# The last pair of chunks of a Strassen-type down projection joins the seven products, and the norms behind it are begun early

## The chip, the cores and the metric

One core of one Trainium2 chip. The metric is the device time of one execution in microseconds (us), the median of several; lower is better. Engines: PE (TensorE, matmuls), DVE (VectorE), ACT (ScalarE), POOL (GpSimd), SP (here only the queue that issues DMAs).

## The reference

One transformer block, S = 1024 tokens, D = 1024, DFF = 2816, in float32:

```python
f = _swiglu(_rmsnorm(x, ffn1_pre_g[l]), ffn1_w_gate[l], ffn1_w_up[l], ffn1_w_down[l])
x = x + 0.5 * _rmsnorm(f, ffn1_post_g[l])
h = _rmsnorm(x, mix_pre_g[l])
qkv = h @ w_qkv[l]
...
x = x + _rmsnorm(heads @ w_out[l], mix_post_g[l])
f = _swiglu(_rmsnorm(x, ffn2_pre_g[l]), ffn2_w_gate[l], ffn2_w_up[l], ffn2_w_down[l])
x = x + 0.5 * _rmsnorm(f, ffn2_post_g[l])
```

where `_swiglu(x, g, u, d) = (silu(x @ g) * (x @ u)) @ d`, and heads come from grouped-query attention and a dilated windowed attention, which the change does not touch.

## The kernel before

Every float32 factor is split into a high part in a short float type (ACT, L118) and a low rest (DVE or POOL, L119), and each product is three passes of matmuls (`PASSES`). The hidden width is cut into NF = 22 chunks of 128. The gate and up projections of a chunk go through seven products of a Strassen-Winograd scheme (P1 to P7, line 289). The down projection does the same over pairs of chunks: a pair j is a 2 x 2 block matrix (two chunks by two halves of the tokens) times a 2 x 2 block matrix of weights (b11, b12, b21, b22: two chunks by two column halves of the output). The seven products k = 0 to 6 of a pair are twelve matmuls 128x512 each, three for each of four rows i of 128 tokens (line 357). The ten pairs are done in two groups of five, all pairs of a group for k = 0, then all for k = 1, and so on, so that a product adds up in PSUM over the pairs of its group. One (k, j) is an *item*. At a group's end of product k its four rows are added into the token tiles y (T = i for the first half of the tokens, i + 4 for the second); `U`, the sum of products 0 and 2, is added into three blocks of y for each row, in the second group by twelve additions that are put off (`late`, L371) and let into DVE's queue one at a time as items are emitted.

For each item two 128x512 blocks are split (L118 and L119 on b, a weight block, and on h, a left block that comes back from DRAM), two items ahead (`WBUFS`). The weight combinations that the products need are made in place by POOL (L260 to L265), after the split that still reads the old block.

Chunks 20 and 21 stay out of the pairs. `tail` (L472) multiplies them plainly, token tile by token tile: twelve matmuls a tile, 96 in all, with T in the order 4, 5, 6, 7, 0, 1, 2, 3. In FFN1 the post norm (L542 to L544), the mixer's pre-norm (`mix_norm`, L480), the transposes into `actT` (L107 to L109) and the first two weights of the qkv projection (L568) run tile by tile behind it; in FFN2 the post norm and the store of the output (L1064) do.

A scheduler orders the instructions on each engine at build time; an engine runs its own in order.

Of the kernel before, what the change touches and what calls it, by code (L numbers as in the profile page):

```python
# [36 lines left out]
def tile_macaron_block(ctx, tc, x, f1_pre, f1_post, f1_g, f1_u, f1_d, mix_pre, mix_post, w_qkv,  # L37
# [83 lines left out]
    class Ffn:  # L121
# [17 lines left out]
        def __init__(self, wg, wu, wd, tag, far):  # L139
# [3 lines left out]
            self.A, self.Hs, self.S = {}, {}, {}  # L143
            self.items = [("G", i, p) for i in range(1, NF) for p in (self.ORDER if i < NF - 1 else self.LAST)]
            downs = [("D", k, j) for g in self.GROUPS for k in range(7) for j in g]
# [4 lines left out]
            self.tiles += [("N", c, d) for d in range(2) for c in range(2)]  # L150
            self.wanted = [d[1:] for d in downs] + [("h", i, h) for i in (NF - 2, NF - 1) for h in range(2)]
# [3 lines left out]
            self.made = self.used = self.done = 0  # L155
# [44 lines left out]
        def feed(self):  # L200

            while self.made < len(self.tiles) and self.made - self.used < self.WBUFS:
                it = self.tiles[self.made]
                self.made += 1
                {"G": self.prepare, "D": self.prepare_down, "N": self.prepare_last}[it[0]](*it[1:])
# [22 lines left out]
        def open_down(self):  # L228

            self.dw = open_pool("dw" + self.tag, bufs=len(self.GROUPS[0]), side=self.far)  # L230
            for j in self.GROUPS[0]:
                self.load_block(j, "b11")

        def load_block(self, j, name):
            c, b = divmod(self.BLOCKS.index(name), 2)
            r = self.B[j, name] = self.dw.tile([128, 512], F32, name=name)
            SP.dma_start(r, self.wd[128 * (2 * j + c):128 * (2 * j + c) + 128, 512 * b:512 * b + 512])
# [9 lines left out]
        def prepare_down(self, k, j, part):  # L247
# [6 lines left out]
            if k == 0 and j in self.GROUPS[0]:  # L254
                for b in ("b21", "b22", "b12"):
                    self.load_block(j, b)
            b11, b12, b21, b22 = [self.B[j, n] for n in self.BLOCKS]
# [8 lines left out]
            if k > 2:  # L266
                after = j + len(self.GROUPS[0])
                if after <= self.PAIRS:
                    self.load_block(after, {3: "b12", 4: "b21", 5: "b11", 6: "b22"}[k])
# [59 lines left out]
        def keep(self, j):  # L329

            a11, a21, a12, a22 = [self.H[2 * j + c][b] for c in range(2) for b in range(2)]
            s2, s3, s4 = [self.dn.tile([128, 512], F32, name="h") for _ in range(3)]
            for k, t in ((0, a11), (1, a12), (4, a22)):
                SP.dma_start(self.hd[k, j], t)
            for k, o, p, q, op in ((5, a21, a21, a22, OP.add), (2, s2, a21, a11, OP.subtract),
                                   (3, s3, a22, s2, OP.subtract), (6, s4, a12, s2, OP.subtract)):
                def made(k=k, o=o, p=p, q=q, op=op):
                    DVE.tensor_tensor(o, p, q, op=op)
                    SP.dma_start(self.hd[k, j], o)
                self.late.append(made)  # L340

        def down(self, k, j, y, ps, psd):
            A, B = [self.W[j, k, z].rearrange("p a k f -> p a (k f)") for z in range(2)]
            g = j in self.GROUPS[1]
            start, end = j == self.GROUPS[g][0], j == self.GROUPS[g][-1]
            first = k in (0, 2, 3, 5)
            U, add, tt = self.U, OP.add, DVE.tensor_tensor
            for i in range(4):
                if first and start:
                    if k in (0, 3):  # L350
                        self.Q[i] = psd.tile([128, 512], F32, name="pd")
                    else:
                        b = "abcd"[i]
                        self.Q[i] = ps[i // 2].tile([128, 4, 128], F32, name="p" + b).rearrange("p t f -> p (t f)")
                p = self.Q[i]
                for n, (a, b) in enumerate(PASSES):
                    PE.matmul(p, A[:, a, 128 * i:128 * i + 128], B[:, b, :],  # L357
                              start=(first and start and n == 0), stop=(end and n == 2), skip_group_check=True)
# [6 lines left out]
                if k == 0:  # L365
                    ACT.activation(U[:, i], p, AF.Copy)
                elif k == 2:
                    tt(U[:, i], U[:, i], p, op=add)
                    if g:
                        for v in (yv(i, 1), yv(i + 4, 0), yv(i + 4, 1)):  # L370
                            self.late.append(lambda v=v, i=i: tt(v, v, U[:, i], op=add))  # L371
                else:
# [5 lines left out]
                    else:  # L378
                        tt(v, U[:, i], p, op=add)

        def split_h(self):

            for i in (NF - 2, NF - 1):
                for half in range(2):
                    src = self.A.pop(("h", i, half))
                    hv, lv = [self.dn.tile([128, 512], FR, name="h") for _ in range(2)]
                    ACT.activation(hv, src, AF.Copy)
                    DVE.tensor_tensor(lv, src, f32(hv), op=OP.subtract)
# [749 lines left out]
```

## Time and profile before

| | |
|---|---|
| median of 3 runs | 2056.73 us (2054.08 to 2058.05) |
| the profiled execution | 2054.44 us, span 2052.7 us |
| mean granted TensorE clock | 0.992 |
| busy: PE, DVE, POOL, ACT | 1978.4, 1338.1, 1056.0, 1005.4 us |
| instructions on PE | 10728 |

The time is that of the whole execution, the span that from the first to the last instruction in the trace. An engine's busy time is the sum over its instructions; the granted clock is a share of full speed.

### The profile page before, as it was taken

Reading aid. Unit: us, or ns where it says so; the run is one execution under the profiler, and the core shown is the slowest. Engines: PE = TensorE matmul, PEld = TensorE weight load, DVE = VectorE, ACT = ScalarE, POOL = GpSimd, SP = SyncE. Lnnn points to the kernel's source line nnn. Section 1 sums busy time; section 2 is a strip of 40 time slices with the busy share of each in tenths; the row PEclk is TensorE's granted clock in tenths of the full one; section 3 lists DMA queues with packets and bytes.
Section 4 is the critical chain, followed back from the end, with each engine's and each line's share of the span. In section 5 each row is a group of like instructions: output and inputs, shape, how many; then the busy total and the mean of one; then the engine's idle time right before and its main releaser. Section 6 shows DMA issues by size and latency. Waiting matters only on the chain. (4 is left out here: it accounts for less than half of the span.)

```text
span 2052.7 us, 30441 instructions
## 1 busy us (share of the span) xinstructions
PE 1978.4 (96%) x10728; PEld 1675.0 (82%) x10728; DVE 1338.1 (65%) x2255; ACT 1005.4 (49%) x1892; POOL 1056.0 (51%) x894
## 2 busy tenths in 40 slices
PE   7999999999999699999999999999999999999995
PEld 6777777787888599998999998887777777778884
DVE  7655454557667846756999888356545445576688
ACT  5433333334444433436999999234333333344443
POOL 4566656666050604234777887315565665651504
PEclk9999999999999899999999999999999999999998
DMA  4233332326532542233040643322223233365434
GB/s 149 76 100 100 106 103 82 124 88 231 185 113 88 200 136 92 73 105 71 1 139 1 205 136 98 103 77 72 93 88 124 86 98 99 101 231 175 123 93 174
DMA packets 210681, 233.01 MB, mean 114 GB/s; under 512 B 21088, under 2 KB 147040, under 8 KB 210400
## 3 DMA queue, kind: packets, MB, share of 16 engines
q1 hardware_dynamic: 210528, 231.06, 35.8%
q8 instruction: 85, 1.39, 0.3%
q14 instruction: 68, 0.56, 0.1%
HBM read 164.95 MB, written 66.06 MB: 113 GB/s over the span
## 5 line engine op out<-in xcount | busy, mean ns | idle before, releaser
L119 POOL TENSOR_TENSOR wgu<-rawgu,wgu 128x512 fp32r<-128x512 f32 x216 | 315.5, 1469 | 354.2 <-ACT wgu L118 332.2
L118 ACT ACTIVATE wgu<-rawgu 128x512 fp32r<-128x512 f32 x302 | 181.7, 627 | 376.9 <-POOL rawgu L226 190.3
L289 PE MATMUL pa<-actT,wgu 128*128 128x512 f32 (+1 forms) x1080 | 268.7, 396 | 9.6 <-ACT U L410 8.7
L357 PE MATMUL pd<-wgu 128*128 128x512 f32 x1140 | 272.4, 391 | 2.5 <-DVE wgu L119 2.2
L357 PEld LDWEIGHTS pd<-wgu 128*128 128x128 f32 x1140 | 213.0, 188 | 51.5 <-DVE wgu L119 5.9
L289 PEld LDWEIGHTS pa<-actT,wgu 128*128 128x128 f32 x1080 | 197.7, 190 | 66.1 <-ACT U L410 21.9
L568 PE MATMUL pq<-wq,actT 128*128 128x256 f32 x1728 | 217.2, 284 | 0.7 <-ACT actT L108 0.7
L568 PEld LDWEIGHTS pq<-wq,actT 128*128 128x128 f32 x1728 | 208.5, 189 | 1.3 <-ACT actT L108 1.0
L118 ACT ACTIVATE wgu<-b 128x512 fp32r<-128x512 f32 x148 | 93.1, 631 | 203.3 <-PE pd L357 113.2
L119 DVE TENSOR_TENSOR wgu<-b,wgu 128x512 fp32r<-128x512 f32 x144 | 118.1, 821 | 98.9 <-ACT wgu L118 98.5
L768 POOL TENSOR_SCALAR P<-P,il 128x1024 f32<-128x1024 f32 (+1 forms) x128 | 130.4, 1018 | 64.9 <-DVE il L767 61.5
L447 DVE TENSOR_TENSOR h<-h,C 64x512 f32<-64x512 f32 x42 | 51.4, 1223 | 161.4 <-ACT h L446 161.3
L869 DVE TENSOR_TENSOR PT<-pt,PT 128x512 fp32r<-128x512 f32 (+1 forms) x256 | 146.3, 614 | 2.0 <-ACT PT L868 2.0
L289 PE MATMUL pd<-actT,wgu 128*128 128x512 f32 x552 | 136.3, 395 | 0.5 <-DVE U L418 0.5
L289 PE MATMUL pc<-actT,wgu 128*128 128x512 f32 x552 | 136.0, 395 | 0.0
L868 ACT ACTIVATE PT<-pt 128x512 fp32r<-128x512 f32 (+1 forms) x256 | 125.1, 543 | 10.7 <-PE pt L865 7.4
L865 PE MATMUL pt<-identr,P 128*128 128x128 f32 x896 | 125.1, 275 | 1.7 <-ACT vst L703 1.1
L289 PEld LDWEIGHTS pd<-actT,wgu 128*128 128x128 f32 x552 | 103.4, 188 | 26.2 <-DVE U L418 1.2
L289 PEld LDWEIGHTS pc<-actT,wgu 128*128 128x128 f32 x552 | 103.4, 188 | 24.9 <-DVE actT L109 0.3
L289 PE MATMUL pc<-tx,wgu 128*128 128x512 f32 x504 | 122.6, 392 | 0.0
L289 PE MATMUL pb<-tx,wgu 128*128 128x512 f32 x504 | 122.4, 391 | 0.0
L289 PE MATMUL pd<-tx,wgu 128*128 128x512 f32 x504 | 121.3, 390 | 0.0
(190 smaller groups left out, 3905.8 us busy)
## 6 DMA issues: line engine op xcount, KB each, us to landing
hd<-h SPq DMA_DIRECT2D x140, 256.0 KB, 2.9
h<-hd SPq DMA_DIRECT2D x140, 256.0 KB, 2.9
rawgu<-in_ffn_w_gate_dram SPq DMA_DIRECT2D x88, 256.0 KB, 3.0
rawgu<-in_ffn_w_up_dram SPq DMA_DIRECT2D x88, 256.0 KB, 3.5
b<-in_ffn_w_down_dram SPq DMA_DIRECT2D x88, 256.0 KB, 3.3
bkT<-kd SPq DMA_DIRECT2D x32, 320.0 KB, 7.5
rawq<-in_w_qkv_dram SPq DMA_DIRECT2D x16, 512.0 KB, 4.8
bV<-vd SPq DMA_DIRECT2D x8, 640.0 KB, 4.0
```

The lines of the kernel that those rows point to most:

```text
L118: ACT.activation(hi, raw, AF.Copy)
L119: return eng.tensor_tensor(lo, raw, f32(hi), op=OP.subtract).ins
L289: PE.matmul(p[:, c0:c1, :], w[:, a, k, :], self.rhs(name, b, k)[:, c0:c1, :], start=(first and n == 0), stop=(n == 11), skip_group_check=True)
L357: PE.matmul(p, A[:, a, 128 * i:128 * i + 128], B[:, b, :], start=(first and start and n == 0), stop=(end and n == 2), skip_group_check=True)
L447: DVE.tensor_tensor(dst, s[64:128], c[64:128], op=OP.mult)
L568: PE.matmul(p, actT[:, a, k, T, :], WQ[j][:, b, k, :], start=(n == 0), stop=(n == 23))
L768: POOL.tensor_scalar(P[:, 0:w], P[:, 0:w], il, 1.0, op0=OP.mult, op1=OP.mult)
L865: PE.transpose(out=p[:, j, :], in_=col(P, b0 + j), identity=ident)
L868: ACT.activation(hv, p[:, 0:n, :], AF.Copy)
L869: DVE.tensor_tensor(lv, p[:, 0:n, :], f32(hv), op=OP.subtract)
```

## The change

The last two chunks become an eleventh pair; the groups have five and six pairs, and the order of the products is 0, 2, 3, 4, 5, 1, 6, so that the second half of the tokens (T = 4 to 7) is finished by product 5, and products 1 and 6 finish the first half. The last two items are done together, row by row, and `row` finishes a row's norm as soon as it is complete. `jobs` puts the norms of tiles 4 to 7 (`post1`, `post2`), the mixer's norm, the split of the first qkv weight and the first transposes behind given items of products 1 and 6. The mixer's gain goes into the qkv weights (`split_mix`: ACT and DVE in place of ACT and POOL). POOL's combinations are made in products 0 and 3 in place of products 0 to 2, for both groups alike. U lives in buffers of the pool u.

```diff
-        LAST = ("P1", "P6", "P7", "P2", "P4", "P5", "P3")
+        LAST = ("P1", "P6", "P7", "P5", "P2", "P4", "P3")
...
-        PAIRS = (NF - 2) // 2
+        PAIRS = NF // 2
+        DOWN = (0, 2, 3, 4, 5, 1, 6)
...
-            downs = [("D", k, j) for g in self.GROUPS for k in range(7) for j in g]
+            downs = [("D", k, j) for g in self.GROUPS for k in self.DOWN for j in g]
...
-            self.split_w((j, k, 1), (b11, b21, b11, b12, b21, b11, b22)[k], DVE)
-            if k == (j in self.GROUPS[0]):
+            self.split_w((j, k, 1), (b11, b21, b11, b12, b12, b11, b22)[k], DVE)
+            if k == 0:
                 tt(b12, b22, b12, op=sub)
-            if k == 1:
                 tt(b11, b12, b11, op=add)
-            if k == 2:
-                tt(b21, b21, b11, op=sub)
+            elif k == 3:
+                tt(b12, b21, b11, op=sub)
                 tt(b11, b22, b11, op=sub)
...
-        def prepare_last(self, c, d):
-            self.split_w(("N", c, d), self.B[self.PAIRS, self.BLOCKS[2 * c + d]], (DVE, POOL)[c])
...
                     if g:
-                        for v in (yv(i, 1), yv(i + 4, 0), yv(i + 4, 1)):
-                            self.late.append(lambda v=v, i=i: tt(v, v, U[:, i], op=add))
+                        for v in (yv(i + 4, 1), yv(i + 4, 0), yv(i, 1)):
+                            self.late.append(lambda v=v, i=i: tt(v, v, U[i], op=add))
...
-                        tt(v, U[:, i], p, op=add)
+                        tt(v, U[i], p, op=add)
+                if row:
+                    row(i)
...
+            last = self.GROUPS[1][-2:]
+            at = self.items.index(("D", 1, self.GROUPS[1][0]))
+            for n, it in enumerate(self.items):
+                if n == at:
+                    self.add_late(len(self.late))
...
+                elif it[1:] == (6, last[0]):
+                    self.down(6, last, y, ps, psd, row)
+                    break
                 else:
-                    self.down(*it[1:], y, ps, psd)
+                    self.down(it[1], it[2:], y, ps, psd)
                     self.used += 2
+                for job in jobs.get(n - at, ()):
+                    job()
...
+    def post_scale(Ts, r, g, xr, dst, done=0):
+
         for n, T in enumerate(Ts):
+            yt = y[:, T, :]
+            if done:
+                DVE.tensor_tensor(yt[:, done:], yt[:, done:], g[:, done:], op=OP.mult)
+                DVE.scalar_tensor_tensor(yt, yt, r[n], xr[n], op0=OP.mult, op1=OP.add)
+            else:
+                DVE.scalar_tensor_tensor(yt, yt, r[n], g, op0=OP.mult, op1=OP.mult)
+                DVE.tensor_tensor(yt, yt, xr[n], op=OP.add)
+            SP.dma_start(dst(T), yt)
...
+    def post_early(T, g):
+
+        if T % 2 == 0:
+            SS[T // 2] = stat.tile([128, 2, 2], F32, name="ss4")
+        yh = y[:, T, 0:512]
+        ACT.activation(actT[:, HI, 0:4, 3], yh.rearrange("p (k f) -> p k f", k=4), AF.Square,
+                       accum_out=SS[T // 2][:, 0, T % 2:T % 2 + 1])
+        POOL.tensor_tensor(yh, yh, g[:, 0:512], op=OP.mult)
...
+        for k in range(raw.shape[1]):
+            g = gm[:, k0 + k:k0 + k + 1]
+            ACT.activation(hi[:, k], raw[:, k], AF.Copy, scale=g)
+            DVE.scalar_tensor_tensor(lo[:, k], raw[:, k], g, f32(hi[:, k]), op0=OP.mult, op1=OP.subtract)
...
+    f1.run((psg0, psg1), y, psd,
+           {0: [begin1, lambda: post1((4, 5))], 3: [lambda: mix1((4, 5))], 4: [lambda: post1((6, 7))],
+            5: [early1], 6: [lambda: mix1((6, 7))], 7: [first_q], 8: [lambda: to_actT(4, y[:, 4, :], psd)],
+            9: [lambda: to_actT(5, y[:, 5, :], psd)]}, row1)
...
+    f2.run((psg0, psg1), y, psd, {0: [begin2, lambda: post2((4, 5))], 4: [lambda: post2((6, 7))], 5: [early2]}, row2)
```

Three places show how the rows of an engine move. The first is POOL in FFN1, second group of pairs, before the change: behind the last combinations of product 2 (L265) come only two splits of the tail's weights and the gain's scaling.

```order
L264 TENSOR_TENSOR b_4341<-b_4341,b_4459 128x512
L265 TENSOR_TENSOR b_4363<-b_4481,b_4363 128x512
L265 TENSOR_TENSOR b_4389<-b_4507,b_4389 128x512
L265 TENSOR_TENSOR b_4415<-b_4529,b_4415 128x512
L265 TENSOR_TENSOR b_4437<-b_4551,b_4437 128x512
L265 TENSOR_TENSOR b_4459<-b_4573,b_4459 128x512
L119 TENSOR_TENSOR wgu<-b_5049,wgu 128x512
```

The same place after the change: the twelve combinations L264 and L265, two for each of the six pairs, each pair behind the split of its b block for product 3 (b_4157, b_4159 and so on).

```order
L262 TENSOR_TENSOR b_4371<-b_4251,b_4371 128x512
L264 TENSOR_TENSOR b_4157<-b_4393,b_4273 128x512
L265 TENSOR_TENSOR b_4273<-b_4509,b_4273 128x512
L264 TENSOR_TENSOR b_4159<-b_4395,b_4275 128x512
L265 TENSOR_TENSOR b_4275<-b_4511,b_4275 128x512
L264 TENSOR_TENSOR b_4185<-b_4421,b_4301 128x512
L265 TENSOR_TENSOR b_4301<-b_4537,b_4301 128x512
```

They have moved from product 2 to product 3. The second is what DVE has in its queue there after the change: the splits of product 3 (L119), the evacuation of product 2 into U (L371), and the additions of U to y (L374).

```order
L119 TENSOR_TENSOR wgu<-b_4157,wgu 128x512
L119 TENSOR_TENSOR wgu<-h,wgu 128x512
L371 TENSOR_TENSOR U_3808<-U_3808,pa 128x512
L371 TENSOR_TENSOR U_3809<-U_3809,pb 128x512
L371 TENSOR_TENSOR C_3810<-C_3810,pc 128x512
L371 TENSOR_TENSOR U_3811<-U_3811,pd 128x512
L119 TENSOR_TENSOR wgu<-b_4159,wgu 128x512
L119 TENSOR_TENSOR wgu<-h,wgu 128x512
L374 TENSOR_TENSOR y<-y,U_3808 128x512
L119 TENSOR_TENSOR wgu<-b_4185,wgu 128x512
L119 TENSOR_TENSOR wgu<-h,wgu 128x512
L374 TENSOR_TENSOR y<-y,U_3808 128x512 x2
```

POOL's L264 on b_4159 may start when DVE's split of b_4159 is through, so it meets the additions that follow. The third is DVE in FFN2 after the change, in product 1 of the second group, where the norm of tiles 4 and 5 (`post2`) stands among the splits for products 1 and 6.

```order
L81 TENSOR_SCALAR rs_b<-ss_19826 128x2
L119 TENSOR_TENSOR wgu<-b_18885,wgu 128x512
L82 RECIPROCAL rs_y<-rs_t 128x2
L86 TENSOR_TENSOR rs_t<-rs_y 128x2
L87 TENSOR_TENSOR rs_t<-rs_t,rs_b 128x2
L88 SCALAR_TENSOR_TENSOR rs_y<-rs_t,rs_y 128x2
L119 TENSOR_TENSOR wgu<-h,wgu 128x512
L534 SCALAR_TENSOR_TENSOR y<-y,rs_y,gpost 128x1024 x2
L535 TENSOR_TENSOR y<-y,xr 128x1024 x2
L119 TENSOR_TENSOR wgu<-b_18907,wgu 128x512
```

Before the change this norm stood behind the last product's splits, among the tail's evacuations (L476).

## Rows read from the trace of the kernel before

**Rows 1.** The page, part 1: busy us (share of the span) and instructions of each engine.

```profile
PE 1978.4 (96%) x10728; PEld 1675.0 (82%) x10728; DVE 1338.1 (65%) x2255; ACT 1005.4 (49%) x1892; POOL 1056.0 (51%) x894
```

**Rows 2.** Timeline at FFN1's end: start us, us, engine, line, operation.

```profile
667.76 16.59 PE L472 MATMUL pd<-wgu,h 128*128 128x512 f32 x72
...
741.64 1.04 PE L107 MATMUL pd<-identr,y 128*128 128x128 f32 x8
...
755.58 19.65 PE L568 MATMUL pq<-wq,actT 128*128 128x256 f32 x164
```

**Rows 3.** Waits of PE, 668 to 775: waited for, us, times, longest.

```profile
PE pd L107 <- DVE y L480: 17.7, 2, 12.8
```

**Rows 4.** Windows: us, busy of PE, PEld, DVE, ACT, POOL; PEclk, DMA, GB/s.

```profile
690.00:700.00 10.00, 2.80 (x11) 2.61 (x12) 9.91 (x7) 1.77 (x4) 9.37 (x4) 0.50 0.00 0
2040.00:2053.00 13.00, 0.00 (x0) 0.00 (x0) 9.14 (x17) 2.91 (x8) 4.92 (x4) 0.50 0.32 122
610.00:640.00 30.00, 29.93 (x133) 24.48 (x132) 25.37 (x42) 12.69 (x22) 0.78 (x1) 1.00 0.37 114
```

**Rows 5.** Timeline at FFN2's end; what ended the idle time before stands in brackets.

```profile
2003.35 0.84 PE L357 MATMUL pa<-wgu 128*128 128x512 f32 x3
2003.55 1.15 ACT L118 ACTIVATE wgu<-b 128x512 fp32r<-128x512 f32 x2 [1.56 <-PE pd L357]
...
2004.22 1.29 DVE L119 TENSOR_TENSOR wgu<-b,wgu 128x512 fp32r<-128x512 f32 x2 [1.43 <-ACT wgu L118]
...
2006.07 0.84 PE L357 MATMUL pa<-wgu 128*128 128x512 f32 x3
...
2008.79 15.24 PE L472 MATMUL pd<-wgu,h 128*128 128x512 f32 x66
...
2048.22 1.42 DVE L1064 SCALAR_TENSOR_TENSOR y<-y,rs_y,xr 128x512 f32<-128x512 f32 x2
```

**Rows 6.** DMA issues: count, KB each, median us from issue to landing.

```profile
out_dram<-y SPq DMA_DIRECT2D x12, 256.0 KB, 2.0
...
out_dram<-y SPq DMA_DIRECT2D x2, 512.0 KB, 2.8
```

**Rows 7.** Timeline 598 to 721: durations of the operations that are moved.

```profile
598.67 2.47 DVE L375 TENSOR_TENSOR y<-y,pd 128x512 f32<-128x512 f32 x4
...
671.51 1.06 ACT L100 ACTIVATE actT<-y 128x1024 fp32r<-128x1024 f32 x1 [2.92 <-DVE y L476]
...
680.92 1.28 DVE L543 SCALAR_TENSOR_TENSOR y<-y,rs_y,xr 128x1024 f32<-128x1024 f32 x1
...
720.42 0.42 DVE L579 TENSOR_TENSOR vst<-pq,vst 128x256 fp32r<-128x256 f32 x1
```

**Rows 8.** Timeline of FFN1, first group, product 1: POOL beside DVE.

```profile
490.80 1.77 DVE L119 TENSOR_TENSOR wgu<-b,wgu 128x512 fp32r<-128x512 f32 x1
491.98 1.74 POOL L260 TENSOR_TENSOR b<-b,b 128x512 f32<-128x512 f32 x1
492.49 1.77 DVE L119 TENSOR_TENSOR wgu<-h,wgu 128x512 fp32r<-128x512 f32 x1
...
496.02 3.02 PE L357 MATMUL pd<-wgu 128*128 128x512 f32 x12 [0.37 <-DVE wgu L119]
...
499.42 2.83 PE L357 MATMUL pd<-wgu 128*128 128x512 f32 x11 [0.38 <-DVE wgu L119]
```

**Rows 9.** Timeline of FFN1's start: the combinations of x beside POOL's split.

```profile
40.34 9.71 DVE L320 TENSOR_TENSOR y<-y 128x512 f32<-128x512 f32 x16
47.38 4.43 POOL L119 TENSOR_TENSOR wgu<-rawgu,wgu 128x512 fp32r<-128x512 f32 x1 [8.33 <-ACT wgu L118]
49.96 0.69 DVE L119 TENSOR_TENSOR wgu<-rawgu,wgu 128x512 fp32r<-128x512 f32 x1
```

**Rows 10.** Timeline of FFN1, second group, products 3 on.

```profile
612.18 28.38 PE L357 MATMUL pd<-wgu 128*128 128x512 f32 x123
...
617.66 1.89 DVE L371 TENSOR_TENSOR y<-y,U 128x512 f32<-128x512 f32 x3
```

More of the change, by code (lines that the diff above doesn't have):

```diff
@@ L342, in down, with made @@
[L342 to L345, printed above, removed]
+            S = {"a11": a11, "a12": a12, "a22": a22, "s1": a21}
+            def made(k, o, p, q, op):
+                if o not in S:
+                    S[o] = self.dn.tile([128, 512], F32, name="h")
+                DVE.tensor_tensor(S[o], S[p], S[q], op=op)
+                SP.dma_start(self.hd[k, j], S[o])
@@ L346, in down @@
+            for z in ((5, "s1", "s1", "a22", OP.add), (2, "s2", "s1", "a11", OP.subtract),
+                      (3, "s3", "a22", "s2", OP.subtract), (6, "s4", "a12", "s2", OP.subtract)):
+                self.late.append(lambda z=z: made(*z))
+        def down(self, k, js, y, ps, psd, row=None):
+            g = js[0] in self.GROUPS[1]
+            start, end = js[0] == self.GROUPS[g][0], js[-1] == self.GROUPS[g][-1]
             first = k in (0, 2, 3, 5)
             U, add, tt = self.U, OP.add, DVE.tensor_tensor
+            Q = self.Q.setdefault(k < 2, {})
@@ L348, in down @@
             for i in range(4):
                 if first and start:
-                    if k in (0, 3):
-                        self.Q[i] = psd.tile([128, 512], F32, name="pd")
-                    else:
[L353 to L358, printed above, removed]
+                    if k == 0:
+                        Q[i] = psd.tile([128, 512], F32, name="pd")
+                    else:
+                        Q[i] = ps[i // 2].tile([128, 4, 128], F32, name="p" + "abcd"[i]).rearrange("p t f -> p (t f)")
@@ L359, in down @@
+                p = Q[i]
+                for j in js:
+                    A, B = [self.W[j, k, z].rearrange("p a k f -> p a (k f)") for z in range(2)]
+                    for n, (a, b) in enumerate(PASSES):
+                        PE.matmul(p, A[:, a, 128 * i:128 * i + 128], B[:, b, :],
+                                  start=(first and start and j == js[0] and n == 0),
+                                  stop=(end and j == js[-1] and n == 2), skip_group_check=True)
                 if not end:
@@ L378, in down @@
                     else:
-                        tt(v, U[:, i], p, op=add)
[L381 to L388, printed above, removed]
-                    self.Hs[i, half] = (hv, lv)
+                        tt(v, U[i], p, op=add)
+                if row:
+                    row(i)
         def add_late(self, n):
@@ L559, in split_q @@
         WQ[j] = w
-        for kk in range(2):
-            split(w[:, HI, 4 * kk:4 * kk + 4, :], w[:, LO, 4 * kk:4 * kk + 4, :], raw[:, 4 * kk:4 * kk + 4, :])
+        split_mix(w[:, HI], w[:, LO], raw, 0)
     def qkv_mm(j, T, ps, bufs=3):
@@ new lines, in first, with turn1 @@
+    def first(j, T):
+        store_v(j, T, qkv_mm(j, T, psq), wq1)
+    def turn1(T):
+        to_actT(T, y[:, T, :], psd)
+    mix1((0, 1))
+    turn1(6)
+    first(0, 4)
+    turn1(7)
+    first(0, 5)
+    mix1((2, 3))
+    split_q(1, wq1, raw1, "wq1")
+    first(0, 6)
+    first(0, 7)
+    raw2 = [f1.dn.tile([128, 2, 256], F32, name="h") for _ in range(4)]
+    for kk in range(4):
+        SP.dma_start(raw2[kk], w_qkv[0][256 * kk:256 * kk + 256, COLS[2]:COLS[2] + 256]
+                     .rearrange("(k p) f -> p k f", p=128))
@@ L632, in tile_macaron_block @@
+    for n in range(4):
+        turn1(n)
+        first(1, 4 + n)
+    for T in range(4):
+        for j in range(2):
+            first(j, T)
     psq.release()
     psd.release()
-    pre.release()
+    wq1.release()
+    E1["wq0"].release()
+    E1["pre"].release()
     ypool.release()
@@ L1070, in tile_macaron_block @@
     f2.w.release()
-    fin.release()
+    E2["fin"].release()
     ypool.release()
```

234 lines of the change are left out of this document (98 added, 136 removed).

## The prediction

> **What bounds the kernel now.** I read the page first: TensorE is busy for 96% of the span and no other engine for more than 65% [rows 1]. So TensorE is the bound almost everywhere, and the change can only win where TensorE waits or works needlessly, or lose where another engine falls behind it. Then I read the timeline at the ends of both feed-forward networks (FFNs), which the change rewrites.
>
> Seam 1 (FFN1 into the projection). The plain tail starts at 667.76, and the first eight transposes after it and the projection follow; the first matmul on the third weight comes at 755.58 + 48 x 0.12 = 761.4 [rows 2], 93.6 us later. Of those, TensorE waits 17.7 us in two pieces for the pre-norm of the mixer, the longer 12.8 [rows 3]. In one 10 us stretch DVE is busy for 9.91 and POOL for 9.37 while TensorE does 2.80, and its granted clock there is 0.50, the lower level (1.2 GHz) [rows 4].
>
> Seam 2 (the end). The tail starts at 2008.79; DVE's last operation ends at 2048.22 + 1.42 = 2049.64 [rows 5]; the span ends at 2052.7, so 43.9 us after the tail began and 3.06 after the last operation, of which 2.0 is the last store's 256 KB [rows 6]. From 2040 on TensorE does nothing [rows 4].
>
> The stretch before seam 1, products 3 to 6 of the second group, is the one to keep in mind: it runs from 612.18 [rows 10] to 667.76 [rows 2], 55.6 us for 20 items. An item (12 matmuls) takes 2006.07 - 2003.35 = 2.72 us [rows 5], so 20 want 54.4: 1.2 us are lost. In 610 to 640 DVE is busy for 25.37 of 30 us, POOL for 0.78 [rows 4]. DVE is the second tightest engine there, and it has room only because POOL is silent.
>
> **The change, part by part.**
>
> *Matmuls.* Twelve fewer in each FFN: 84 instead of 96, 84 x 0.2267 (2.72/12) = 19.0 us for the last pair.
>
> *Seam 1.* If TensorE never waited, the same work would be 19.0, 64 transposes at 1.04/8 = 8.3, and 16 x 24 = 384 projection matmuls at 19.65/164 = 0.12, 46.3 [rows 2]: 73.6 us against 93.6, a gain of 20. But the norms of tiles 4 to 7 now stand in DVE's queue in the last two products (1 and 6), between the weight splits for which TensorE waits. What DVE does there: 22 splits at 0.6 (two take 1.29, [rows 5]) = 13.2; 8 evacuations at 0.6 (four take 2.47, [rows 7]) = 4.8; two pairs of norms, each four 128x1024 operations at 1.2 (1.28 long, [rows 7], the start overlapping its predecessor) and 0.9 of small ones = 11.4; a wait of 0.9 on ACT's square root and square (the square takes 1.06, [rows 7]); and four POOL multiplications that block DVE at 1.1 = 4.4. That is 34.7. In FFN1 come 8 pieces of the weight split at 0.34 (from the 0.42 of a 128x256 subtraction, [rows 7], less the overlap) = 2.7, two short chains for the mixer's norm = 1.8, and four evacuations of transposes = 2.4: 41.6. All of it stands ahead of the splits for the double last item, which starts after ten items, at 27.2. A split is ready at 2004.22 + 1.29 = 2005.51 and wanted by the item's second matmul at 2006.07 + 0.23, so it may be 0.8 late [rows 5]. Bound: 41.6 - 27.2 - 0.8 = 13.6 of stall; below, 0 if the small operations slip into gaps. I take 12, as DVE's order is fixed and 1.6 of short chains can hide under waits. Net gain 8 (0 to 20).
>
> *Seam 2.* The stall is 34.7 - 27.2 - 0.8 = 6.7 by the same sum. Behind the last matmul four rows are left: each 0.6 evacuation, 0.6 multiplication by the gain, 1.2 for scale and residual, and 0.9 of small ones = 3.3, 13.2 for four. The first row's sum is complete three rows (3 x 1.36 = 4.1) ahead of the last, and 1.4 goes by until its evacuation and square are through: 13.2 - 4.1 + 1.4 = 10.5. Then the last store, now 512 KB: 2.8 [rows 6] and the 1.06 that remains of the 3.06. So 19.0 + 6.7 + 10.5 + 3.9 = 40.1 against 43.9: gain 4 (0 to 10).
>
> *POOL's combinations and the late additions.* The edit that moves L264 and L265 from product 2 to product 3 is, I think, the dear one. In the second group before, they were over when the twelve additions y += U of product 2 (L371 before, three of them in 1.89 us [rows 10], L374 after) entered DVE's queue; now twelve of them lie under these additions. What the two engines do to each other shows where both have work: DVE's subtractions on SBUF operands take 1.77 instead of the 0.69 of [rows 9], and POOL's combination 1.74; the items there start 499.42 - 496.02 = 3.40 apart, each with a wait on L119 [rows 8]. So a POOL operation under a loaded DVE costs DVE 1.1. In product 3 of the second group, after its first split, DVE has 22 operations with two SBUF operands, 8 evacuations and one more split = 31 x 0.6 = 18.6, and ten POOL operations (two of the twelve run under the four evacuations from PSUM, which a POOL operation does not hold up): 18.6 + 11 = 29.6, where seven items (19.0) and the slack of 0.8 allow 19.8. Loss 9.8 instead of the 1.2 of now: 8.6 in each FFN. In the first group the same move costs 1.3, because items of that group already run 3.40 apart beside POOL's combinations [rows 8], which pays for most of it. Together 2 x (8.6 + 1.3) = 20. Lower bound 0, if POOL does not get in (the rival below); upper bound 2 x 13.2 = 26, if all twelve cost 1.1.
>
> The Trainium skill (SBUF — State Buffer, Who interferes with whom) says that a DVE operation with two SBUF inputs and a GpSimd operation that reads SBUF exclude each other whole, and that issue order decides who waits. The trace agrees in [rows 8] (1.77 and 1.74) and not in [rows 9]; by that rule the sum stays as below, by [rows 9] it would be 2042.
>
> *Edits at nothing.* The mixer's gain in the weights (8 small operations per later weight) lies in the projection, where TensorE is the bound; its 1,024 four-byte elements load long before. The reordering P5 before P2, the separate block pools and the stores of tiles 4 to 7 ahead of the last two loads are covered by the loads' lead of four items (AHEAD), 4 x 2.72 = 10.9 us; without the cover a late load of 256 KB would cost the 2.0 of [rows 6].
>
> *Sum.* 2054.44 (the profiled run, 2.3 below the median of 2056.73) - 8 - 4 + 20 = 2062.4, so 2062.
>
> **The rivals.** 0.2% (4.1 us) is about what a measurement can tell.
>
> A, DVE keeps the port (faster). For 16 additions in a row, 9.71 us, DVE ran undisturbed and the next subtraction at 49.96 too; POOL's operation, started at 47.38, took 4.43 [rows 9]. If U's additions do the same, POOL's combinations slip behind them to where DVE has gaps (it needs them only for product 4), and the 20 vanishes: 2054.4 - 12 = 2042. Against it: the additions stand in runs of one to three between splits (the order of the change), and splits do let POOL in [rows 8]. It decides from the point where POOL gets fewer than two operations in before each run ends. A half-way case, 10 instead of 20, is 2052 to 2057: no change, or nearly none.
>
> B, the stalls in the last two products are larger. TensorE waits in pieces of 3 to 6 us, as it did for the mixer's norm [rows 3], and the clock goes to 0.50 as in [rows 4]: another 8 to 12 above the forecast, 2070 to 2074.
>
> C, the norms do not really begin earlier (the transposes of tiles 4 and 5 wait for the mixer's chain, which waits for ACT): seam 1 as now, about 2071.
>
> **How the numbers follow.** Forecast 2062 (2056 to 2069): 0.46. A: 0.32. Half-way: 0.08. B: 0.10. C: 0.04. The range 2040 to 2077 takes in A and B. Faster by over 0.2% is A and a little of the half-way case: 0.34; within it, half-way and the lower edge of the forecast: 0.10; slower 0.56.
>
> **What would show it.** Right: in product 3 of the second group items of 3.4 us and more, TensorE waiting on L119, L374 and L119 of 1.7 us beside L264 and L265 of 1.6 or more, and DVE full from there on. Seam 1 with waits of some 12 us inside products 1 and 6, none of the 12.8 kind. End: some 14 us from the last matmul. Wrong: L374 at 0.6 throughout and POOL operations of 3 us or more (rival A), or TensorE idle for more than 13 us in the last two products of FFN1, at a clock of 0.50 (rival B).

## The result and the profile after

The changed kernel takes 2066.14 us (median of four runs, 2065.26 to 2070.95), the kernel before, on the same chip, 2056.28 (four runs, 2054.08 to 2058.05). The ratio is 1.0051, with an interval of 1.0039 to 1.0064: slower by half a per cent. The profiled execution took 2066.44 with a span of 2064.7, against 2054.44 and 2052.7 before, so 12.0 us are to be found in the trace. The medians are only 9.9 apart: the traced execution of the kernel before is 1.8 below its median, so about 2 of the 12 are spread between executions. The mean granted clock is 0.992 in both.

The page's first part answers to [rows 1]:

```profile
PE 1986.9 (96%) x10704; PEld 1676.6 (81%) x10704; DVE 1353.2 (66%) x2323; ACT 1030.1 (50%) x1977; POOL 995.4 (48%) x864
```

TensorE has 24 matmuls fewer and is yet busy for 8.5 us more: some of its matmuls are longer, and the rows below show where. The place to begin is the list of waits. From 470 to 725, FFN1's down phase, it stands like this (waited for, us in all, times, the longest):

```profile
PE pa L359 <- DVE wgu L119: 7.6, 6, 2.1
PE pd L107 <- DVE y L378: 5.0, 1, 5.0
PE pa L359 <- DVE y L382: 3.0, 1, 3.0
PE pd L359 <- DVE wgu L119: 2.9, 1, 2.9
PE pa L359 <- DVE y L378: 2.4, 1, 2.4
```

In the kernel before, the waits of the same phase up to the plain tail were these, 1.7 us in all:

```profile
PE pd L357 <- DVE wgu L119: 1.4, 4, 0.5
PE pa L357 <- DVE wgu L119: 0.3, 1, 0.3
```

All the lines name DVE, before and after. What it is late with are splits (L119) and evacuations (L378, L382), the operations that add a finished product from PSUM into y. Of the first line's 7.6 us 6.3 lie in product 3 of the second group, and so does the last line, at its end. The timeline of this product (start us, us, engine, line, operation; the idle time before and what ended it in brackets):

```profile
612.25 1.68 POOL L264 TENSOR_TENSOR b<-b,b 128x512 f32<-128x512 f32 x1 [0.62 <-DVE wgu L119]
612.70 1.78 DVE L374 TENSOR_TENSOR y<-y,U 128x512 f32<-128x512 f32 x1
614.01 1.62 POOL L265 TENSOR_TENSOR b<-b,b 128x512 f32<-128x512 f32 x1
614.40 1.78 DVE L119 TENSOR_TENSOR wgu<-b,wgu 128x512 fp32r<-128x512 f32 x1
...
616.26 1.68 POOL L264 TENSOR_TENSOR b<-b,b 128x512 f32<-128x512 f32 x1 [0.63 <-DVE wgu L119]
616.71 4.07 DVE L374 TENSOR_TENSOR y<-y,U 128x512 f32<-128x512 f32 x3
618.01 1.62 POOL L265 TENSOR_TENSOR b<-b,b 128x512 f32<-128x512 f32 x1
618.90 0.39 PE L359 MATMUL pa<-wgu 128*128 128x512 f32 x1
620.70 0.68 DVE L119 TENSOR_TENSOR wgu<-b,wgu 128x512 fp32r<-128x512 f32 x1
...
621.43 0.74 PE L359 MATMUL pa<-wgu 128*128 128x512 f32 x2 [2.14 <-DVE wgu L119]
...
624.10 0.39 PE L359 MATMUL pa<-wgu 128*128 128x512 f32 x1
...
636.51 1.25 PE L359 MATMUL pa<-wgu 128*128 128x512 f32 x3 [2.44 <-DVE y L378]
637.56 1.48 PE L359 MATMUL pb<-wgu 128*128 128x512 f32 x3
...
640.93 0.85 PE L359 MATMUL pa<-wgu 128*128 128x512 f32 x3
```

A run of three additions took 1.89 before [rows 10] and takes 4.07 now, with two POOL operations beside it. A single addition or split beside one takes 1.78 instead of 0.68. The next split (620.70) is so late that TensorE waits 2.14 for it, and an item lasts 624.10 - 618.90 = 5.2 us instead of 2.72. Five pairs of L264 and L265 stand between 612 and 635 in this manner: ten blocked operations. The item behind the last wait (636.51 to 640.93) takes 4.42: its groups of three matmuls take up to 1.48 instead of 0.85.

Windows (us, busy of PE, PEld, DVE, ACT, POOL; clock, DMA, GB/s) of product 3, of the item behind it, of a piece of the last two products (1 and 6), of those two products whole in FFN1 and FFN2, and of the end:

```profile
609.84:636.51 26.67, 17.91 (x72) 13.12 (x73) 26.67 (x27) 8.06 (x14) 18.17 (x12) 1.00 0.20 60
637.00:639.00 2.00, 2.00 (x6) 1.50 (x6) 2.00 (x4) 0.00 (x0) 0.00 (x0) 0.50 0.28 100
680.00:690.00 10.00, 7.08 (x24) 5.41 (x23) 9.02 (x21) 9.68 (x19) 0.00 (x0) 0.83 0.77 265
671.13:717.04 45.91, 38.03 (x162) 30.63 (x160) 41.44 (x75) 36.51 (x71) 6.43 (x5) 0.93 0.52 179
2012.43:2052.00 39.57, 35.69 (x145) 27.61 (x143) 34.89 (x61) 22.24 (x46) 7.14 (x4) 0.96 0.39 152
2052.00:2064.70 12.70, 0.00 (x0) 0.00 (x0) 8.63 (x21) 2.04 (x6) 0.00 (x0) 0.69 0.40 165
```

In the first DVE is busy for every one of its 26.67 us, and POOL for 18.17. The 72 matmuls are six items, 16.3 us of work: 10.4 are lost. The second shows the item behind the wait at a granted clock of 0.50, the lower level (1.2 GHz). The last two windows answer to the end in [rows 4, 5]: behind the last matmul 12.7 us are left.

At FFN1's end, where [rows 2, 3] stood, the trace of the change shows:

```profile
677.87 2.47 DVE L534 SCALAR_TENSOR_TENSOR y<-y,rs_y,gpost 128x1024 f32<-128x1024 f32 x2
680.26 2.35 DVE L535 TENSOR_TENSOR y<-y,xr 128x1024 f32<-128x1024 f32 x2
682.53 0.68 DVE L119 TENSOR_TENSOR wgu<-b,wgu 128x512 fp32r<-128x512 f32 x1
683.27 9.17 PE L359 MATMUL pd<-wgu 128*128 128x512 f32 x32 [2.92 <-DVE wgu L119]
...
702.35 1.12 PE L107 MATMUL pd<-identr,y 128*128 128x128 f32 x4 [4.96 <-DVE y L378]
...
742.03 58.19 PE L595 MATMUL pq<-wq,actT 128*128 128x256 f32 x492
```

Four norm operations stand ahead of the split that TensorE waits 2.92 for, and the transposes at 702.35 wait 4.96. The wait of 12.8 of [rows 3] is gone.

**Where the 12 us lie.** From each stretch, before and after, I take off what TensorE needs for its items at 2.72 each, and compare what is left. Products 1 and 6 now come last and contain five items of pairs that stood ahead of the tail before; these five are taken off in the rows of the last two products, which therefore hold the same work as the tail had, less the twelve matmuls saved.

| stretch | predicted | measured |
| --- | --- | --- |
| FFN1, start of the down phase up to product 3 of the second group | +1.3 | +4.1 |
| FFN1, products 3 to 6 before; 3, 4 and 5 after | +8.6 | +11.8 |
| FFN1, the tail or the last two products, and the projection up to its third weight | -8 | -16.4 |
| FFN2, the same first stretch | +1.3 | +4.1 |
| FFN2, products 3 to 6 before; 3, 4 and 5 after | +8.6 | +10.2 |
| FFN2, the tail or the last two products, to the end | -4 | -5.2 |
| everything else | 0 | +3.4 |
| sum | +8 | +12 |

### The profile page after: what moved, and what is told of

Its sections match the earlier page's. It is cut to its first block, busy times and chain, and to the rows that moved or that the text cites. A ratio compares the mean times of both kernels' runs of the same rounds, so it can differ in the third digit from the quotient of the medians.

```text
span 2064.7 us, 30519 instructions
## 1 busy us (share of the span) xinstructions
PE 1986.9 (96%) x10704; PEld 1676.6 (81%) x10704; DVE 1353.2 (66%) x2323; ACT 1030.1 (50%) x1977; POOL 995.4 (48%) x864
## 5 line engine op out<-in xcount | busy, mean ns | idle before, releaser
L119 POOL TENSOR_TENSOR wgu<-rawgu,wgu 128x512 fp32r<-128x512 f32 x216 | 313.4, 1460 | 362.1 <-ACT wgu L118 334.7
L359 PE MATMUL pd<-wgu 128*128 128x512 f32 x858 | 218.6, 396 | 7.3 <-DVE wgu L119 7.3
L119 DVE TENSOR_TENSOR wgu<-b,wgu 128x512 fp32r<-128x512 f32 x154 | 128.2, 833 | 109.8 <-ACT wgu L118 109.4
L359 PEld LDWEIGHTS pd<-wgu 128*128 128x128 f32 x858 | 164.0, 192 | 44.5 <-DVE wgu L119 9.4
L921 ACT ACTIVATE PT<-pt 128x512 fp32r<-128x512 f32 (+1 forms) x256 | 125.2, 544 | 13.6 <-PE pt L918 10.1
L119 DVE TENSOR_TENSOR wgu<-h,wgu 128x512 fp32r<-128x512 f32 x154 | 126.2, 820 | 1.8 <-ACT wgu L118 1.8
L359 PE MATMUL pa<-wgu 128*128 128x512 f32 x330 | 100.8, 404 | 23.6 <-DVE wgu L119 14.0
```

The source lines that it names most:

```text
L119: return eng.tensor_tensor(lo, raw, f32(hi), op=OP.subtract).ins
L359: PE.matmul(p, A[:, a, 128 * i:128 * i + 128], B[:, b, :], start=(first and start and j == js[0] and n == 0), stop=(end and j == js[-1] an ...
L921: ACT.activation(hv, p[:, 0:n, :], AF.Copy)
```

## The experiments

Each kernel is the changed one with the edit shown. The first ten were timed in one execution each, the last two in five rounds; the kernel before, on the same chips, took 2054 to 2057 us (medians). The four timed executions of the changed kernel lie 5.7 us apart, so one single time says little about differences below that; for those I go by the traces.

**1. No combinations by POOL in the second group.** Two of them, L264 and L265, leave the program, so products 4 to 6 multiply other numbers; the work of TensorE stays.

```
-            elif k == 3:
+            elif k == 3 and j < n:
```

> The changed kernel without POOL's twelve combinations L264 and L265 in the second group of each FFN (left out, so products 4 to 6 of that group multiply by the old blocks). Theory (port): the twelve combinations are what makes DVE's two-operand instructions 1.7 us long there, so all of L374 and L119 in product 3 of the second group fall to 0.7, its six items take about 17.5 us instead of 26.7, no wait of TensorE over 1 us is left in it, and the time falls by 2 x 10 to 2 x 12, to about 2044. Rival (DVE is simply full: twelve additions more than the stretch holds, whatever POOL does): the stretch stays at 23 us or more and the time above 2058.

It took 2045.16, 21.0 less, as expected: it takes back the loss of the second groups, for which the prediction had 2 x 9.8. Timeline rows of its product 3:

```profile
612.18 1.89 DVE L374 TENSOR_TENSOR y<-y,U 128x512 f32<-128x512 f32 x3
...
613.98 0.69 DVE L119 TENSOR_TENSOR wgu<-b,wgu 128x512 fp32r<-128x512 f32 x1
```

The three additions take 1.89 again and a split 0.69, as before, with the same work in DVE's queue. The product takes 16.6 us, and between 600 and 640 TensorE waits for nothing.

**2. No additions of U in the second group.** This leaves the twelve additions out and keeps POOL's operations.

```
-                    if g:
-                        for v in (yv(i + 4, 1), yv(i + 4, 0), yv(i, 1)):
-                            self.late.append(lambda v=v, i=i: tt(v, v, U[i], op=add))
```

> The changed kernel without the twelve additions of U in the second group of each FFN (left out, so three blocks of y a row lack U). Theory (port): the combinations still lengthen every split to 1.7; 19 DVE operations x 0.6 + 10 x 1.1 = 22.4 against 19.8, as in the first group, where six us were lost with no additions: product 3 of the second group takes 19 to 22 us instead of 26.7, the time is about 2054 (2050 to 2058). Rival (DVE is simply full): without the additions nothing waits, the stretch takes 16.5 us and the time is 2042 to 2046.

It took 2059.6, 1.6 above the upper bound. Rows of product 3:

```profile
617.14 1.78 DVE L119 TENSOR_TENSOR wgu<-b,wgu 128x512 fp32r<-128x512 f32 x1
618.45 1.62 POOL L265 TENSOR_TENSOR b<-b,b 128x512 f32<-128x512 f32 x1
618.84 1.77 DVE L119 TENSOR_TENSOR wgu<-h,wgu 128x512 fp32r<-128x512 f32 x1
```

With the additions gone POOL blocks the splits instead, and each blocked one again costs 1.1. Product 3 takes 20.7 us, inside the expected 19 to 22, but it ends in a wait of 2.98 and an item of 5.26 at the lower clock (granted 0.50 from 629 to 631), which I had not counted. So DVE is not simply full of additions, which would have left no wait: the two engines together are the cost.

**3. The additions one product later.** They are queued behind the evacuation of product 3 and run in products 4 and 5. Nothing is left out.

```
-                            self.late.append(lambda v=v, i=i: tt(v, v, U[i], op=add))
+                            self.late.append(lambda v=v, i=i: self.add_u(v, U[i]))
...
+        def add_u(self, v, u):
+            with tc.issue_after(self.evac):
+                DVE.tensor_tensor(v, v, u, op=OP.add)
```

> Complete computation; the twelve additions of U in the second group are queued behind the evacuation of product 3, so that they lie in products 4 and 5, where POOL is silent (six in each, at DVE's queue places after the splits). Theory (port): as without the additions, product 3 at 19 to 22 us, the additions at 0.6 in products 4 and 5 cost at most 1: 2054 to 2058. Rival (DVE is full wherever they lie): the loss only moves to products 4 and 5 and the time stays at 2062 or more.

It took 2053.65, just under the expected 2054 to 2058, where the kernel before took 2055.68 beside it: the loss against it is gone. Product 3 lasts 20.66 us, as in experiment 2:

```profile
606.86:627.52 20.66, 17.22 (x72) 13.27 (x73) 19.84 (x17) 8.07 (x14) 18.27 (x12) 1.00 0.29 77
```

POOL's 18.27 us are unchanged. The additions go into products 4 and 5, where POOL is silent, and from the wait at the end of product 3 (2.9) on TensorE waits for nothing up to 660. That the time is 6 us below that of experiment 2, with a product 3 of the same length, is not the additions' doing: 2.5 of it lie in FFN1's last two products and the projection behind them, which both programs have alike up to the third weight (97.9 us against 95.5). Single runs differ by that much.

**4. L265 emitted one product later.**

```
-                tt(b11, b22, b11, op=sub)
-            elif k in (1, 4, 5, 6) and j < n:
+            if k == 4:
+                tt(b11, b22, b11, op=sub)
+            if k in (1, 4, 5, 6) and j < n:
```

> Complete computation; L265 (b11 = b22 - b11), which only product 5 needs, is made in product 4 instead of product 3, in both groups: POOL has six combinations in product 3 and six in product 4. Theory (port): five or six blocks of 1.1 us fewer in product 3: in the second group 26.7 falls to 19 to 22, in the first group the 6 us lost fall to 2 or 3; product 4 has few two-operand instructions beside its splits and loses under 1. The time falls by 2 x 8, to about 2050 (2046 to 2055). Rival (DVE is full by itself): no change within 3 us of 2066.

It took 2065.14, outside the expected 2046 to 2055, with the same waits. The scheduler had left POOL's order as it was, since the operation depends on nothing later. So the run tests nothing of the theory; it is a second sample of the change.

**5. L265 held behind the last L264 of its group**, with the wait that experiment 4 lacked.

```
+                self.l264 = tt(b12, b21, b11, op=sub).ins
+            if k == 4:
+                with tc.issue_after(self.l264):
+                    tt(b11, b22, b11, op=sub)
```

> Complete computation; as the run e4_l265_later, whose edit left POOL's order as it was, but with L265 of every pair queued behind the last L264 of its group, so that POOL has six (first group: five) combinations in product 3 and six (five) from its end on. Theory (port): product 3 of the second group loses 4 to 6 us instead of 12, product 4 loses 2 or 3, the first group 3 instead of 7: about 2050 (2045 to 2056). Rival (the number of combinations in the stretch does not matter, one blocked instruction in the chain of split and wait is enough): above 2060.

It took 2062.43, outside the expected 2045 to 2056: a miss, and where the rival had put it (above 2060). Rows of product 3 and behind it:

```profile
612.35 2.99 DVE L376 TENSOR_TENSOR y<-y,U 128x512 f32<-128x512 f32 x3
...
625.27 9.79 POOL L267 TENSOR_TENSOR b<-b,b 128x512 f32<-128x512 f32 x6
625.79 1.76 DVE L119 TENSOR_TENSOR wgu<-b,wgu 128x512 fp32r<-128x512 f32 x1
```

A run of three additions now takes 2.99, one blocked operation instead of two. But the six L265 (L267 in this kernel) follow one another for 9.79 us from the end of product 3 on and block splits for product 4. In product 3 seven DVE operations are blocked instead of ten, and it takes 23.3 us instead of 26.7: 3.4 less, three times 1.1. So the number does matter, against the rival; but two more operations are blocked at the start of product 4, nine in all, and in FFN2 product 4 gives 2.7 of the gain back. The edit spares hardly any blocked operation, so it could not gain much.

**6. Experiments 5 and 3 together.**

> Complete computation; L265 behind the last L264 as in e5_l265_behind, and the additions of U in products 4 and 5 as in e3_adds_later. Theory (port): the two gains add up, product 3 of the second group loses under 2 us, product 4 has six combinations and six additions and loses 2 to 4: about 2040 (2035 to 2047). Rival: the same loss turns up in product 4, 2050 or more.

It took 2048.53, 1.5 above the expected range and below the rival's 2050. Together the two edits gain 17.6; apart they gained 3.7 and 12.5, which is 16.2, the same within the spread. Product 3 takes 18.5 us.

**7. The additions later, and DVE does the combinations itself**, in both groups.

```
-                tt(b12, b21, b11, op=sub)
-                tt(b11, b22, b11, op=sub)
+                DVE.tensor_tensor(b12, b21, b11, op=sub)
+                DVE.tensor_tensor(b11, b22, b11, op=sub)
```

> Complete computation; as e3_adds_later, and DVE makes the combinations L264 and L265 itself, in both groups, so that POOL is silent in product 3. Theory (port): twelve operations of 0.6 more on DVE instead of twelve blocks of 1.1: 31 x 0.6 = 18.6 against 19.8, product 3 of the second group loses under 1.5 us, that of the first 28 x 0.6 = 16.8 against 14.4, 2 to 3: about 2034 (2029 to 2041). Rival (DVE is full by itself): more work on DVE makes it slower than e3_adds_later, 2058 or more.

It took 2047.17, 6 above the expected range: the direction was right, the size was not. Product 3, and one combination in it:

```profile
605.75:622.50 16.75, 16.13 (x71) 13.13 (x71) 16.56 (x28) 6.92 (x12) 0.00 (x0) 1.00 0.34 95
```
```profile
609.74 0.69 DVE L264 TENSOR_TENSOR b<-b,b 128x512 f32<-128x512 f32 x1
```

Six items in 16.75 us: the loss of this product is gone, though DVE has twelve operations more, at 0.69 each. The two down phases together are 11.6 us shorter than in experiment 3, where I had expected some 20: I had taken the whole loss of the first group for recoverable, 7.7 us in FFN1, and 2.1 of these lie in products 0 and 2, which the edit does not touch. The times differ by only 6.5, since this run's first down phase began 2.2 later and 2.5 more went by between the two down phases; no run here shows why.

**8. DVE does the combinations, and nothing else is changed.**

> Complete computation; the changed kernel with one edit: DVE makes L264 and L265 itself, in both groups; six of the U additions stay in product 3 of the second group. Theory (port): twelve operations of 0.6 cost DVE less than twelve blocks of 1.1; DVE's sum there is 12 combinations, 11 splits, 6 additions and 8 evacuations, 37 x 0.6 = 22.2 against 19.8: 2 to 3 us lost instead of 12, and 4 instead of 7.7 in the first group: about 2050 (2045 to 2056). Rival (DVE's load as such, not the port, makes the loss): twelve operations more on the full engine, above 2066.

It took 2051.35, as expected. Taking POOL out of the contention is worth 14.8 us, though the work moves to the engine that is full. The rival that DVE's load as such were the cause (above 2066) falls. In the first group of FFN1 the wait for L382 shrinks from 3.0 to 0.8. In the second one long wait is left, for the evacuation of product 3:

```profile
PE pa L359 <- DVE y L378: 2.8, 1, 2.8
```

**9. FFN2's norms of tiles 4 to 7 only after the last row.**

```
-    f2.run((psg0, psg1), y, psd, {0: [begin2, lambda: post2((4, 5))], 4: [lambda: post2((6, 7))], 5: [early2]}, row2)
+    f2.run((psg0, psg1), y, psd, {0: [begin2], 5: [early2]}, row2)
+    post2((4, 5))
+    post2((6, 7))
```

> Complete computation; the changed kernel, with the norms of tiles 4 to 7 of FFN2 done after its last row instead of inside products 1 and 6. My sum: the stall in the last two products falls from 6.9 to about 1, and behind the last matmul come two pairs of norms, 11.4 us, more: 2066 - 6 + 11 = 2071 (2068 to 2075). Rival (norms inside the products cost as much as they save, since they put TensorE to its lower clock): 2062 to 2067.

It took 2071.74, as expected. The waits of TensorE from 1995 on, which in the changed kernel are 3.7 us with one of 3.2:

```profile
PE pa L359 <- DVE wgu L119: 0.4, 1, 0.4
PE pd L359 <- DVE wgu L119: 0.2, 1, 0.2
```

The stall in the last two products goes (the down phase shortens from 234.7 to 229.2), but the norms then stand at the end: 22.7 us are left behind the last matmul instead of 12.7. By the two traces the early norms earn 10.0 and cost 5.5.

**10. FFN1's transposes of tiles 4 and 5 behind the last row.**

```
-            5: [early1], 6: [lambda: mix1((6, 7))], 7: [first_q], 8: [lambda: to_actT(4, y[:, 4, :], psd)],
-            9: [lambda: to_actT(5, y[:, 5, :], psd)]}, row1)
+            5: [early1], 6: [lambda: mix1((6, 7))], 7: [first_q]}, row1)
...
+    with tc.issue_after(f1.end):
+        for T in (4, 5):
+            turn1(T)
```

> Complete computation; the changed kernel with the transposes of tiles 4 and 5 (FFN1) queued behind the last row instead of behind items of product 6. If the 5.0 us that TensorE waits for L378 there is a matter of their place (they need the PSUM buffers that product 1's evacuation, stuck behind DVE's norm and weight split, frees late), the wait shrinks to 1 to 3 us behind the last row, and the time falls by 2 to 5, to about 2063. If it is a matter of DVE's load, the same wait comes back at the first projection matmuls: 2065 to 2067.

It took 2070.57 where 2063, or 2065 to 2067, was expected: a miss. The time alone lies within the spread of the changed kernel, but the trace shows a loss: from the start of product 1 to the projection's third weight it takes 102.3 us instead of 96.4. The wait of 5.0 on the transposes came back as one on a split:

```profile
PE pa L359 <- DVE wgu L119: 6.9, 1, 6.9
PE pd L359 <- DVE wgu L119: 2.9, 1, 2.9
PE pd L107 <- DVE actT L109: 1.5, 2, 1.3
```

DVE's queue shows why:

```profile
693.61 3.48 DVE L534 SCALAR_TENSOR_TENSOR y<-y,rs_y,gpost 128x1024 f32<-128x1024 f32 x2
697.02 2.35 DVE L535 TENSOR_TENSOR y<-y,xr 128x1024 f32<-128x1024 f32 x2
...
699.88 0.68 DVE L119 TENSOR_TENSOR wgu<-b,wgu 128x512 fp32r<-128x512 f32 x1
```

The split that TensorE wants stands behind 5.8 us of norms. The transposes only showed the stall: what TensorE waits for is whatever stands behind the norms in DVE's queue. With the transposes out of the way it waits longer in one piece, and the transposes come on top behind the last row.

**11 and 12. Two versions that might beat both.** The first joins experiment 7, experiment 10, the multiplication of the early halves by the gain on DVE instead of POOL, and FFN2's scaling of one tile for each item instead of two at once. The second leaves FFN1's end as in experiment 7 and has only the two edits at FFN2's end:

```
-    f2.run((psg0, psg1), y, psd, {0: [begin2, lambda: post2((4, 5))], 4: [lambda: post2((6, 7))], 5: [early2]}, row2)
+    f2.run((psg0, psg1), y, psd, {0: [begin2, lambda: post2((4, 5))], 1: [lambda: scale2(4)], 2: [lambda: scale2(5)], 3: [lambda: post2((6, 7))],
+                               4: [lambda: scale2(6)], 5: [lambda: scale2(7)], 7: [early2]}, row2)
```

> Complete computation; e7_dve_combos with three edits in the last two products: DVE in place of POOL multiplies the first halves of tiles 0 to 3 by the gain (both FFNs), the norm of a tile in FFN2 is given to DVE one tile an item, and the transposes of tiles 4 and 5 stand behind the last row as in e12_turns_late. Theory: the waits of 2.4 and 1.1 beside POOL's multiplications and the one of 3.2 behind the pair of norms in FFN2 go, and 2 at the transposes: 2047 - 8 = 2039 (2034 to 2045), faster than the kernel before by 0.6 to 1%. Rival (the last two products are bound by DVE's total): 2045 to 2049.

> Complete computation; e7_dve_combos with the two edits of e11_best in FFN2 alone (DVE in place of POOL multiplies the first halves of tiles 0 to 3, and the norm of tiles 4 to 7 is given to DVE one tile an item); FFN1 as in e7_dve_combos, with its transposes where the change put them. From the profiles: e11_best needed 231.8 us for the down phase of FFN1 and 231.2 from there to the end of the projection, e7_dve_combos 230.5 and 228.3, 4.2 less; FFN2's down phase took 224.8 in e11_best and 227.3 in e7_dve_combos. So 2042.4 - 4 = 2038 (2035 to 2043). Rival (the transposes' place does not matter and the difference is the spread of single runs): 2041 to 2044.

The first took 2042.36 (ratio to before 0.9928, 0.9915 to 0.9942), the second 2039.87 (0.9921, 0.9906 to 0.9935). Both are in the expected range, and faster than the kernel before and than the change. Their intervals overlap, so the times do not settle whether the transposes' place matters; the traces do. From the start of product 1 to the third weight the first takes 101.5 us and the second 97.9. The eleven traces of the change and its variants with the transposes inside product 6 have 95.5 to 98.2, the two with the transposes behind the last row 101.5 and 102.3. The edits in FFN2 pay a little: its last two products take 38.8 us in the first and 37.7 in the second, against 39.2 to 41.2 in the traces with two tiles at once. How much of that is the norms' spreading and how much DVE's multiplication by the gain is not separated. Waits of the second at FFN1's end:

```profile
PE pd L107 <- DVE y L378: 5.0, 1, 5.0
PE pd L359 <- DVE wgu L119: 2.9, 1, 2.9
```

These 7.9 us still stand there; no run here removes them.

## Why the prediction was right, point by point

It said 2062, slower; 2066.14 came. The mechanism it chose as likeliest is what happened, but the terms were further off than the sum. POOL's combinations were to cost 20, at most 26; the stretches that hold them lost 30.2. The seams were to give back 12 and gave 21.6. These two errors nearly cancel, and that the total came within 4 us is in part luck. The figures that were off are the clock behind the waits, the first group, the base of seam 1, and the parts outside.

**The combinations under the additions (right, size off).** The prediction gave product 3 a loss of 9.8, with ten POOL operations at 1.1 each. The trace has ten blocked operations, 10.4 lost in the product, and then 1.7 that was not in the sum: the item behind the wait of 2.44 ran at the lower clock. The 1.2 that the prediction took as lost before was 0.5: the row that begins at 612.18 [rows 10] holds 123 matmuls, three of them of the product before, and product 3 began at 612.87. Experiments 1 and 8 take away POOL's part and get 21.0 and 14.8 us back; experiment 2 takes away the additions and the splits are blocked in their place. Contention of the two engines is shown, by both sides of it.

**The first group (the step that failed most in proportion).** "In the first group the same move costs 1.3", because its items already ran 3.40 apart [rows 8]. Measured: 4.1 in each FFN. The list of waits names 3.0 of it in one piece, at the start of product 4 for an evacuation (L382); the item behind it again took 4.42. The timeline of FFN1 there:

```profile
520.61 1.38 PE L359 MATMUL pa<-wgu 128*128 128x512 f32 x3 [2.97 <-DVE y L382]
...
525.03 0.85 PE L359 MATMUL pa<-wgu 128*128 128x512 f32 x3
```

The cover that the prediction counted on was smaller than it took it to be: before, the pace of 3.40 held for some items only, and the five items of product 1 took 15.2 us and those of product 2 14.3, 2.2 over 2.72 each together. After, product 2 takes 15.8 and product 3 17.3, 5.9 over. Experiment 8, in which DVE makes the combinations, has 15.2 in product 3.

**Seam 1 (right in kind, the kernel before misread).** The prediction took 755.58 + 48 x 0.12 = 761.4 as the first matmul on the third weight. Between 707.59 and 755.58 there are only six groups of 48 projection matmuls, as the timeline of the kernel before shows (the first and the last of the six):

```profile
707.59 5.94 PE L568 MATMUL pq<-wq,actT 128*128 128x256 f32 x48
...
749.01 5.94 PE L568 MATMUL pq<-wq,actT 128*128 128x256 f32 x48
```

Of the 384 projection matmuls of the first two weights 288 stand ahead of 755.58 and 96 behind: 755.58 + 96 x 0.12 = 767.1, so the seam took 99.3 before, not 93.6. The same point now lies at 742.03 + 216 x 0.1183 = 767.6 (168 of the 384 run ahead of 742.03, the rest at 58.19/492 each). From 671.13 that is 96.5, of which five items (13.6) stood ahead of the tail before: 82.9 for the same work, 16.4 less. The stall inside the last two products was forecast at 12 and is 11.2: 45.9 less twelve items (32.6) and sixteen transposes (2.1). So the gain of 16.4 instead of 8 is the base (5.7), the stall (0.8) and, for the remaining 1.9, the transposes: eight of them were priced at 1.04, and take 0.79 from start to start (730.00 to 730.79), 2.0 less for 64. DVE was busy for 41.4 of the 45.9 us, near the 41.6 of the prediction, but the prediction put the whole stall down to waiting for DVE's queue; in the trace 7.9 of the 11.2 are waits (2.92 and 4.96), and the rest is TensorE working slower, with a mean granted clock of 0.93.

**Seam 2 (right).** Forecast: stall 6.7, 40.1 in all, a gain of 4. Measured: 39.55 - 32.6 = 6.9, 52.3 - 13.6 = 38.7, a gain of 5.2. The last rows took 12.7 instead of 14.4 behind the last matmul. Experiment 9, which undoes the early norms, agrees with both.

**The rivals.** A, that DVE keeps the port through its runs of additions, did not occur: POOL came in twice in the run of three and in each run of two. B occurred only in part: the clock did fall to 0.50 in FFN1's last two products, from 702.3 to 705 behind the wait of 4.96, but it is 0.83 from 680 to 690 and 0.93 over the whole, and the stall there was no longer than forecast. C did not occur: the 12.8 wait is gone.

**What stays open.** 3.4 us lie outside the stretches that the prediction priced: 1.0 in a later start of FFN1's down phase and 2.4 between the projection's third weight and FFN2's down phase, mostly in attention, whose steps on TensorE come 5.53 apart instead of 5.44. The start of the down phase lies anywhere from 471.1 to 473.8 in runs that are alike up to there, so the 1.0 is spread. The steps are 5.49 in six and 5.53 in seven of the thirteen traces of the change and its variants, and 5.44 in the one trace of the kernel before. So 0.04 of the difference is spread; whether the rest belongs to the change, no run here shows.

## What to carry to other kernels

Price an operation that is moved to a helper engine by what it takes from the busy engine beside it (here 1.1 us of DVE for each POOL operation that meets one with two SBUF operands), not by its own engine's idle time. Where that is more than the operation costs on the busy engine itself (0.69 here), give it to the busy engine, even a full one: experiment 8 got 15 us that way. And a wait of TensorE can cost more than its length: behind those of 2.44 and 2.97 us that ended a product in FFN1 the next item took 4.42 instead of 2.72. It need not: behind the wait of 2.14 inside product 3 the granted clock stayed at 1.00, and behind the wait of 3.0 for L382 in FFN2 all five items of product 4 took 13.9 us, 2.78 each. Look at the items behind a wait before pricing it.

## What was not expected of the hardware

POOL came in between DVE additions with SBUF operands: a run of three (1.89 alone) took 4.07 with two POOL operations in it, while POOL's own stretched only to 1.6 to 1.7, from 1.30 beside evacuations (L265 at 610.33). The evacuations, which read one operand from PSUM, took 0.68 beside it and were not held up. In [rows 9] sixteen subtractions in a row kept POOL waiting, with one operation of 4.43, though each of them reads two blocks of y in SBUF (line 320 of the kernel before). The operations differ in what else they read and write, and no run here tells which difference decides.

Six POOL combinations one after the other take 9.79 us beside a busy DVE (1.63 each), and the splits beside them 1.76: spread out or bunched, the price of a blocked operation is the same. Two of the six blocked nothing, since DVE was at its evacuations meanwhile.
